# A gated-DeltaNet and Fourier layer in fp32: the scans' state update as 64-row products, in place of one product over a zero-padded operand

## The chip, the cores and the metric

One core of one Trainium2 chip runs the whole layer in one launch. The metric is the device time of that launch in microseconds, as the median of several runs.

## The reference, cut to what matters

The layer joins a bidirectional gated DeltaNet group (4 heads, head size 128) and a Fourier group, and ends in a SwiGLU FFN. It runs on 2048 sample tokens and 128 prompt tokens. The part that the change touches is the scan over chunks of 64 tokens, run forward and backward:

```python
def step(s, inp):
    u_v_c, w_c, qg_c, aqk_c, kd_c, gl_c = inp
    u = u_v_c - jnp.einsum('bhck,bhkv->bhcv', w_c, s)
    o = jnp.einsum('bhck,bhkv->bhcv', qg_c, s) + jnp.einsum('bhij,bhjv->bhiv', aqk_c, u)
    s = gl_c[..., None, None] * s + jnp.einsum('bhck,bhcv->bhkv', kd_c, u)
    return s, o
```

Per head, the state `s` is 128 x 128; the last product sums over the 64 tokens of a chunk. There are 32 chunks of the sample and 2 of the prompt, in each of two directions.

## The kernel before

`phase_ab` makes projections, convolutions and the per-chunk operands, and leaves them in DRAM. `scan1` and `scan2` run the scans, `phase_d` the FFN. A framework records the operations, then a scheduler orders them on each engine by its own model, and adds the semaphore waits; so the order in the program text is not the order on the engines.

**The scans.** `steps` goes through the steps: 2 over the prompt, 16 in `scan1`, 16 in `scan2`. One step takes one chunk of the forward direction (d = 0) and one of the backward direction (d = 1). `chunk_step` loads the chunk's operands (`pk` holds keys, queries, values and `kt`, the keys with tokens on the partitions; `ab` and `tb` are block-diagonal tiles for two heads) and returns two generators `pair(q)`. A pair is two heads, laid side by side on the 128 partitions: tokens of the first head on partitions 0 to 63 (`lo`), of the second on 64 to 127 (`hi`). `steps` advances the four generators of a step stage by stage, and after each stage calls `beside`, which records some of the other work that runs next to the scans (the Fourier transforms in `scan1`, the output projection in `scan2`); after the step `fill` records a piece of the triangular inversion.

**One pair.** It has one PSUM bank `ps` of tag `m` (four such banks exist, and a step takes all four), cut into `b0`, `b1`, `bu` and `bo` of 128 columns each.

- Stage 1: two products of the states with keys and queries into `b0` and `b1`; DVE makes `r` from them, ACT makes the first part of the output (`part`).
- Stage 2: the product `bu` from `tb` and `r`; ACT copies it out as `u`, and, scaled by `ed`, into the padded operand `rd`.
- Stage 3: the state product of `kt` and `rd` into `b0` and `b1` together, the product `bo` of `ab` and `u`; DVE forms the new states (`S`) and adds `bo` to the output.

The padded operand is one of the tiles `bd[d, "r", q]` (`bd0r`, `bd1r` in the profile), 128 x 2 x 128. The scaled `u` of the first head fills the `lo` half of its first 128 columns, that of the second head the `hi` half of its second 128 columns, and the rest stays zero from a memset at the start of `scan1`. So one product with the 128 rows of `kt` gives both heads' updates:

```python
self.act(rd[lo, 0], bu[lo], AF.Copy, scale=ed[lo])
self.act(rd[hi, 1], bu[hi], AF.Copy, scale=ed[hi])
...
self.mm(ps[:, :2 * P], kt[:, q], rd.rearrange("p h v -> p (h v)"))
```

All operations go through helpers, so the profile gives the helpers' lines: L124 is every product (`mm`), L127 a transpose, L130 `tensor_tensor`, L137 `scalar_tensor_tensor` (`r` and `S`), L140 every ACT operation, L849 and L854 the memsets of the `bd` tiles and of the states.

## Time and profile before

| what | value |
|---|---|
| runs (three) | median 2767.01 us, 2766.07 to 2773.3 |
| the profiled execution | 2767.64 us, its span 2765.8 us |
| granted TensorE clock | 0.971 of full speed over the span |
| busy | PE 94%, PEld 86%, DVE 71%, ACT 50%, POOL 13% |
| DMA | 390.83 MB, mean 141 GB/s |
| the scans | about 756 to 1263 us of the span |

The profile is of one execution. PE is the product itself, PEld the loading of its stationary operand, which runs beside products. A product over fp32 operands shows as two rows each (two passes). The ends of products are modelled, their starts are recorded; so the distance between two starts says what a product took, and a busy share near 100% says only that products followed each other.

### The profile page before, as it was taken

What the parts mean: (1) busy time and instruction counts of PE and PEld (TensorE: products, weight loads), DVE (VectorE), ACT (ScalarE), POOL (GpSimd) and SP (SyncE); (2) the same over time, 40 slices, a digit from 0 to 9 for tenths busy, and PEclk for the clock granted to TensorE, in tenths of its full rate; (3) what the DMA queues carried; (4) which work ended last, traced back from release to release, by engine and by line L of the source; (5) the groups of instructions that cost most, each with busy time, mean ns of one, the idle gap of its engine ahead of it and who ended that gap; (6) DMA issues with size and microseconds to landing.
All of it is one profiled execution on the core that took longest, in us unless ns stands there. A gap on an engine that the chain in (4) does not pass through costs nothing.

```text
span 2765.8 us, 44580 instructions
## 1 busy us (share of the span) xinstructions
PE 2610.3 (94%) x15769; PEld 2366.6 (86%) x15769; DVE 1971.7 (71%) x3860; ACT 1395.2 (50%) x3090; POOL 354.4 (13%) x486
## 2 busy tenths in 40 slices
PE   6999798899999899997999999999999999999998
PEld 3898687788888778876999998789999888999987
DVE  6335598998999677755877766577777556888744
ACT  7756454432277877765433344433434444444442
POOL 1214333431200012220000000020000002000001
PEclk8999898899999999998999999999999999999999
DMA  9946685555365666644322223532222253332342
GB/s 311 307 139 204 177 256 162 157 164 180 109 193 194 195 176 195 200 152 151 90 73 73 73 71 94 179 122 77 73 69 70 89 158 120 105 88 82 95 137 93
DMA packets 412283, 390.83 MB, mean 141 GB/s; under 512 B 99948, under 2 KB 335900, under 8 KB 411164
## 3 DMA queue, kind: packets, MB, share of 16 engines
q1 hardware_dynamic: 323996, 300.92, 36.1%
q10 hardware_dynamic: 74128, 40.13, 5.0%
q0 software_dynamic: 13936, 46.93, 4.9%
q8 instruction: 125, 2.05, 0.3%
q14 instruction: 98, 0.80, 0.1%
HBM read 293.55 MB, written 94.33 MB: 140 GB/s over the span
## 4 chain that ended last, share of the span: by engine, by line
issue 31%; PE 27%; DMA 2%; DVE 1%; ACT 1%; POOL 1%; ACTq 0%; POOLq 0%; SPq 0%; DVEq 0%
PE acc L124 9%; PE m L124 8%; PE acc L1273 5%; PE m L1273 5%; PE tr L127 1%; POOL rstd L130 1%; DMA z_s<-z_d 0%; DMA y_f<-half_d 0%; DMA half_d<-gy 0%; DVE x_f L137 0%; ACT h L140 0%; DVE x_f L130 0%; DMA bd1a<-a_d 0%; POOL y L1401 0%; DMA g<-gate_d 0%
## 5 line engine op out<-in xcount | busy, mean ns | idle before, releaser
L1273 PE MATMUL m<-h,wh 128*128 128x384 f32 (+1 forms) x1848 | 456.1, 329 | 14.5 <-ACT h L140 7.2
L1273 PE MATMUL acc<-h,wh 128*128 128x384 f32 (+1 forms) x1848 | 449.8, 327 | 0.0
L140 ACT ACTIVATE wh<-S 128x512 fp32r<-128x512 f32 x264 | 163.8, 630 | 376.5 <-DVE S L130 161.5
L124 PE MATMUL acc<-hb,w_in 128*128 128x258 f32 (+1 forms) x2304 | 333.6, 302 | 15.7 <-DMA hb<-hT 10.9
L1273 PEld LDWEIGHTS m<-h,wh 128*128 128x128 f32 x1848 | 328.4, 189 | 19.6 <-ACT h L140 8.9
L124 PEld LDWEIGHTS acc<-hb,w_in 128*128 128x128 f32 x2304 | 318.3, 199 | 26.8 <-issue 12.2
L1273 PEld LDWEIGHTS acc<-h,wh 128*128 128x128 f32 x1848 | 327.2, 189 | 1.0 <-ACT wh L140 0.4
L1273 PE MATMUL acc<-h,wl 128*128 128x384 f32 (+1 forms) x924 | 300.6, 327 | 6.0 <-DVE wl L130 6.0
L1273 PE MATMUL m<-h,wl 128*128 128x384 f32 (+1 forms) x924 | 302.3, 328 | 0.0
L140 ACT ACTIVATE wh<-w_gu 128x512 fp32r<-128x512 f32 x198 | 124.4, 630 | 118.8 <-issue 51.6
L130 DVE TENSOR_TENSOR wl<-S,wh 128x512 fp32r<-128x512 f32 x264 | 179.0, 686 | 5.3 <-ACT wh L140 3.1
L1273 PEld LDWEIGHTS acc<-h,wl 128*128 128x128 f32 x924 | 174.0, 189 | 6.9 <-DVE wl L130 6.9
L1273 PEld LDWEIGHTS m<-h,wl 128*128 128x128 f32 x924 | 174.9, 189 | 0.0
L140 ACT ACTIVATE awh<-a 128x384 fp32r<-128x384 f32 x176 | 90.7, 520 | 136.0 <-PE m L124 88.1
L130 DVE TENSOR_TENSOR awl<-a,awh 128x384 fp32r<-128x384 f32 x176 | 96.6, 555 | 87.1 <-ACT awh L140 87.0
L1387 POOL DMA_DIRECT2D half_d<-gy x17 | 9.3, 546 | 1160.9 <-DVE gy L130 1160.3
L130 DVE TENSOR_TENSOR wl<-w_gu,wh 128x512 fp32r<-128x512 f32 x198 | 135.4, 685 | 27.2 <-ACT wh L140 27.0
L130 DVE TENSOR_TENSOR S<-w_gu 128x512 f32<-128x512 f32 x132 | 91.1, 691 | 88.4 <-DMA w_gu<-w_gu 87.9
L137 DVE SCALAR_TENSOR_TENSOR y<-conv_in,wconv,y 128x256 f32<-128x256 f32 (+1 forms) x216 | 123.2, 584 | 39.7 <-ACT conv_in L140 39.1
L130 POOL TENSOR_TENSOR w_ada<-w_raw,w_ada 128x512 fp32r<-128x512 f32 x64 | 99.2, 1566 | 136.9 <-ACT w_ada L140 136.7
L124 PE MATMUL acc<-woh,mh 128*128 128x512 f32 x272 | 113.2, 419 | 3.0 <-DVE gx L130 2.9
L130 DVE TENSOR_TENSOR inv_b<-inv_b,inv_m 128x62 f32<-128x62 f32 (+30 forms) x124 | 114.1, 920 | 2.3
(281 smaller groups left out, 5927.9 us busy)
## 6 DMA issues: line engine op xcount, KB each, us to landing
w_gu<-w_gu SPq DMA_DIRECT2D x264, 256.0 KB
pk<-pk_d SPq DMA_DIRECT2D x68, 512.0 KB
w_dn<-w_down SPq DMA_DIRECT2D x132, 256.0 KB
hb<-hT SPq DMA_DIRECT2D x104, 258.0 KB
w_raw<-w_ada SPq DMA_DIRECT2D x32, 512.0 KB
x<-x SPq DMA_DIRECT2D x17, 512.0 KB
hT<-hi ACTq DMA_DIRECT2D x17, 512.0 KB
hT<-lo POOLq DMA_DIRECT2D x17, 512.0 KB, 6.1
```

The source lines that it names most:

```text
L124: self.nc.tensor.matmul(out, lhsT=lhsT, rhs=rhs, start=start, stop=stop)
L127: self.nc.tensor.transpose(out=out, in_=in_, identity=self.c("ident")[:in_.shape[0], :in_.shape[0]])
L130: (eng or self.nc.vector).tensor_tensor(out=out, in0=a, in1=b, op=op)
L137: self.nc.vector.scalar_tensor_tensor(out=out, in0=a, scalar=s, in1=b, op0=op0, op1=op1)
L140: self.nc.scalar.activation(out=out, in_=in_, func=f, **kw)
L1273: nc.tensor.matmul(o, lhsT=w_[:, ws], rhs=h_[:, k, :sub], start=start and k == i == 0, stop=k == 3 and i == 2, skip_group_check=not start)
L1387: nc.gpsimd.dma_start(self.half_d[n], tmp)
```

## The change

The state product is split by head. ACT now writes one unpadded 128 x 128 tile `rd`. Two products of 64 rows follow, one per head: the first takes partitions 0 to 63 of `kt` and `rd`, the second partitions 64 to 127, so that each uses one half of the array's rows. They write different banks: `grown` takes, for both pairs of a direction, the first head's result from the bank of the first pair and the second head's from the bank of the second pair, at the columns `b0` for the first pair and `b1` for the second. The product `bo`, the new states and the output's additions move into a fourth stage. `steps` runs four stages, and calls `beside` after the first three as before. The padded tiles and their four memsets are gone.

```diff
@@ -843,7 +843,7 @@
         self.ts(self.e2, self.qs, P * EPS, ALU.mult, P * EPS * 1e-6, ALU.add)
         self.bd = {}
         for d in range(2):
-            for kind, count, m in (("a", 3, 2), ("t", 2, 4), ("r", 2, 2)):
+            for kind, count, m in (("a", 3, 2), ("t", 2, 4)):
                 for n in range(count):
                     t = self.bd[d, kind, n] = oacc.tile([P, m, P], F32, name=f"bd{d}{kind}{n}")
                     nc.gpsimd.memset(t, 0.0)
@@ -882,10 +882,11 @@
 
         for slot, *cs in steps:
             heads = [h for d, c in enumerate(cs) for h in self.chunk_step(d, c, slot)]
-            for stage in range(3):
+            for stage in range(4):
                 for h in heads:
                     next(h, None)
-                self.beside(us[stage])
+                if stage < 3:
+                    self.beside(us[stage])
             self.fill(8.0)
 
     def chunk_step(self, d, c, slot):
@@ -912,9 +913,12 @@
         o = self.o_tiles[c]
         lo, hi = slice(0, CH), slice(CH, P)
 
+        banks = []
+
         def pair(q):
             s0, s1 = self.states[d, 2 * q], self.states[d, 2 * q + 1]
             ps = self.bank("m")
+            banks.append(ps)
             b0, b1, bu, bo = (ps[:, i * P:(i + 1) * P] for i in range(4))
             self.mm(b0, kq[:, q, 0], s0)
             self.mm(b1, kq[:, q, 1], s1)
@@ -929,14 +933,16 @@
             yield
             self.mm(bu, tb[:, q], r)
             u = sp.tile([P, P], F32, tag=f"u{d}{q}", name="u", bufs=1)
-            ed, rd = self.ed[:, d, q, c:c + 1], self.bd[d, "r", q]
-            self.act(rd[lo, 0], bu[lo], AF.Copy, scale=ed[lo])
-            self.act(rd[hi, 1], bu[hi], AF.Copy, scale=ed[hi])
+            rd = sp.tile([P, P], F32, tag=f"rd{d}{q}", name="rd", bufs=1)
+            self.act(rd, bu, AF.Copy, scale=self.ed[:, d, q, c:c + 1])
             self.act(u, bu)
             yield
-            self.mm(ps[:, :2 * P], kt[:, q], rd.rearrange("p h v -> p (h v)"))
+            grown = [bank[:, q * P:(q + 1) * P] for bank in banks]
+            for dst, hs in zip(grown, (lo, hi)):
+                self.mm(dst, kt[hs, q], rd[hs])
+            yield
             self.mm(bo, ab[:, q], u)
-            for h2, (st, src) in enumerate(((s0, b0), (s1, b1))):
+            for h2, (st, src) in enumerate(zip((s0, s1), grown)):
                 new = sp.tile([P, P], F32, tag=f"S{d}{2 * q + h2}", name="S")
                 self.stt(new, st, self.gl[:, h2, d, q, c:c + 1], src, ALU.mult, ALU.add)
                 self.states[d, 2 * q + h2] = new
```

The scheduler's order of PE in one step of `scan2`, with buffer numbers. Before: `m_11908` is the bank of direction 0's first pair, `m_11917` that of its second; `bd0r0` and `bd0r1` are their padded operands, `acc` the output projection that runs beside.

```order
L124 MATMUL m_11908<-bd0r0_8494,pk_11900 128x256 [waits Activation_49]
L124 MATMUL m_11908<-u_12009,bd0a0_8484 128x128 [waits DMAHW2_49,DMAHW1_49]
L124 MATMUL acc_12191<-woh4_9739,mh_11972 128x512 [waits DVE_49]
L124 MATMUL acc_12191<-wol4_9747,mh_11972 128x512
L124 MATMUL acc_12191<-woh4_9739,ml_11973 128x512
L124 MATMUL acc_12191<-woh5_9740,mh_11972 128x512
L124 MATMUL acc_12191<-wol5_9748,mh_11972 128x512
L124 MATMUL m_11917<-bd0r1_8496,pk_11900 128x256 [waits Activation_49]
L124 MATMUL m_11917<-u_12014,bd0a0_8484 128x128
```

Of the change, in a step of `scan2`: `m_11992` is the bank of the first pair, `m_12001` of the second; `rd_12094` belongs to the first pair, `rd_12099` to the second. What goes to `m_11992` is a first head's product, what goes to `m_12001` a second head's; `tr` are transposes beside.

```order
L124 MATMUL m_11992<-rd_12099,pk_11984 128x128 [waits Activation_49]
L124 MATMUL m_12001<-rd_12094,pk_11984 128x128 [waits Activation_49]
L124 MATMUL m_12001<-rd_12099,pk_11984 128x128
L124 MATMUL m_11992<-u_12093,bd0a0_8484 128x128 [waits DMAHW5_49,DMAHW3_49]
L127 MATMUL tr_12264<-const_all_73,xn_12153 128x128
L124 MATMUL acc_12279<-wol0_9775,mh_12056 128x512
L124 MATMUL m_12019<-r_12022,bd1t0_8500 128x128 [waits DVE_49,Activation_49]
L124 MATMUL m_12010<-rd_12104,pk_11988 128x128 [waits Activation_49]
```

One product with its `bo` behind it has become two first halves apart from each other (that of the first pair stands some ten rows further up), two second halves in a row behind the second pair's `u`, and `bo` of the first pair behind all of them.

DVE at the same places, the new states `S` and the output `o`. Before:

```order
L137 SCALAR_TENSOR_TENSOR S_12054<-S_11835,gl_2171,m_11908 128x128 [waits PE_49]
L137 SCALAR_TENSOR_TENSOR S_12056<-S_11837,gl_2171,m_11908 128x128
L130 TENSOR_TENSOR o_10025<-o_10025,m_11908 128x128
L137 SCALAR_TENSOR_TENSOR S_12062<-S_11843,gl_2171,m_11917 128x128 [waits PE_49]
L137 SCALAR_TENSOR_TENSOR S_12064<-S_11845,gl_2171,m_11917 128x128
L130 TENSOR_TENSOR o_10025<-o_10025,m_11917 128x128
```

The change:

```order
L137 SCALAR_TENSOR_TENSOR S_12182<-S_11959,gl_2171,m_12001 128x128 [waits PE_49,Activation_49]
L137 SCALAR_TENSOR_TENSOR S_12180<-S_11957,gl_2171,m_11992 128x128 [waits PE_49]
L130 TENSOR_TENSOR o_10065<-o_10065,m_11992 128x128
L137 SCALAR_TENSOR_TENSOR S_12187<-S_11964,gl_2171,m_11992 128x128
L134 TENSOR_SCALAR h_12147<-tr_12264,mod_cols_81 128x128 [waits PE_49]
L134 TENSOR_SCALAR h_12147<-tr_12264,mod_cols_81 128x128
L130 TENSOR_TENSOR gx_12156<-acc_12279,g1_11320 128x512 [waits PE_49]
L130 TENSOR_TENSOR ml_12507<-mf_12508,mh_12506 128x512 [waits DMAHW3_49,Activation_49]
L130 TENSOR_TENSOR x_c_12062<-x_c_12062,gx_12156 128x512 [waits DVE_49]
L137 SCALAR_TENSOR_TENSOR S_12189<-S_11966,gl_2171,m_12001 128x128 [waits PE_49]
L130 TENSOR_TENSOR o_10065<-o_10065,m_12001 128x128
```

The states of one pair came in a row, each pair from its own bank; now the second head's state of the first pair comes first, and the last state, `S_12189`, waits for a later product of PE.

PE between the two, in the change: `u_12098` is the second pair's `u`.

```order
L124 MATMUL acc_12384<-woh4_9771,mh_12283 128x512
L124 MATMUL acc_12384<-wol4_9779,mh_12283 128x512
L124 MATMUL acc_12384<-woh4_9771,ml_12284 128x512
L124 MATMUL acc_12384<-woh5_9772,mh_12283 128x512
L124 MATMUL acc_12384<-wol5_9780,mh_12283 128x512
L124 MATMUL m_12001<-u_12098,bd0a0_8484 128x128 [waits DVE_49]
```

Its product `bo` waits for DVE, which has to read a state's update out of the same bank first; before, this product had no wait on DVE.

## Rows read from the trace of the kernel before

**Rows 1.** Page, section 1: busy us of each engine (share of the span) xinstructions.

```profile
PE 2610.3 (94%) x15769; PEld 2366.6 (86%) x15769; DVE 1971.7 (71%) x3860; ACT 1395.2 (50%) x3090; POOL 354.4 (13%) x486
```

**Rows 2.** Scan stretch by window: length, busy PE, PEld, DVE, ACT, POOL (x), clock, DMA, GB/s.

```profile
756.00:800.00 44.00, 36.38 (x242) 33.06 (x243) 40.85 (x83) 28.56 (x80) 5.63 (x15) 0.92 0.76 209
800.00:870.00 70.00, 67.57 (x465) 60.52 (x464) 68.28 (x168) 54.39 (x154) 0.22 (x1) 1.00 0.60 186
870.00:960.00 90.00, 82.29 (x518) 70.56 (x518) 66.86 (x205) 79.89 (x217) 1.43 (x2) 1.00 0.66 207
960.00:1020.00 60.00, 52.25 (x294) 43.74 (x292) 41.90 (x136) 44.47 (x133) 8.01 (x16) 0.97 0.62 170
1020.00:1200.00 180.00, 178.48 (x1004) 154.58 (x1005) 124.78 (x374) 134.39 (x397) 43.48 (x84) 1.00 0.61 188
```

**Rows 3.** By window, of instructions on `bd0r` alone: PE, PEld, ACT, POOL.

```profile
870.00:1020.00 150.00, 17.09 (x52) 8.24 (x52) 18.83 (x52) 0.00 (x0) 0.99 0.65 192
980.00:1015.00 35.00, 5.57 (x18) 2.81 (x18) 5.44 (x15) 0.00 (x0) 1.00 0.74 205
1050.00:1190.00 140.00, 8.31 (x28) 5.12 (x28) 10.54 (x30) 0.00 (x0) 1.00 0.63 193
```

**Rows 4.** Timeline of PE: start us, length us, line, output<-inputs, weights, moving, passes.

```profile
803.29 0.60 PE L124 MATMUL m<-bd1r,pk 128*128 128x256 f32 x2
803.72 0.38 PE L124 MATMUL m<-u,bd1a 128*128 128x128 f32 x2
...
804.39 0.83 PE L124 MATMUL acc<-w_fno,const_fourier 128*128 128x128 f32 x6
805.06 0.39 PE L124 MATMUL m<-r,bd0t 128*128 128x128 f32 x2
805.38 0.63 PE L124 MATMUL tr<-const_fourier,uv 32*128 32x32 f32 x4
805.93 0.49 PE L124 MATMUL m<-r,bd0t 128*128 128x128 f32 x2
806.26 0.61 PE L124 MATMUL m<-S,pk 128*128 128x128 f32 x4
```

**Rows 5.** The same, around a product with 32 columns of weights.

```profile
843.17 0.61 PE L124 MATMUL acc<-const_fourier,uv 128*128 128x128 f32 x4
843.71 0.65 PE L124 MATMUL tr<-cw,rc 128*32 128x256 f32 x2
844.29 0.49 PE L124 MATMUL acc<-const_fourier,uv 128*128 128x128 f32 x2
```

**Rows 6.** Groups by form, 756 to 1263: xcount | busy us, mean ns | idle before.

```profile
L137 DVE SCALAR_TENSOR_TENSOR S<-S,gl,m 128x128 f32<-128x128 f32 x272 | 81.9, 341 | 17.7 <-PE m L124 6.0 <-ACT o L140 4.0 <-ACT u L140 1.9
...
L140 ACT ACTIVATE bd0r<-m,ed 64x128 f32<-64x128 f32 x136 | 49.2, 362 | 12.6 <-PE m L124 9.8 <-PE acc L124 0.6
...
L124 PE MATMUL m<-bd0r,pk 128*128 128x256 f32 x136 | 42.5, 394 | 5.5 <-ACT u L140 5.2
...
L140 ACT ACTIVATE u<-m 128x128 f32<-128x128 f32 x136 | 37.8, 278 | 1.9
```

**Rows 7.** Timeline of PE, products of column halves (`m<-kq`).

```profile
259.02 1.15 PE L124 MATMUL m<-kq 128*64 128x128 f32 x24
260.11 0.40 PE L124 MATMUL m<-w_ada,cs 128*4 128x512 f32 x1
```

**Rows 8.** Timeline of PE behind a wait, in a bare step.

```profile
940.52 0.70 PE L124 MATMUL m<-bd0r,pk 128*128 128x256 f32 x2 [0.26 <-ACT u L140]
941.06 0.38 PE L124 MATMUL m<-u,bd0a 128*128 128x128 f32 x2
```

**Rows 9.** Tile `pk`, 756 to 1263: engines idle before its instructions until, us, times.

```profile
  ACT u L140: 21.3, 46
```

**Rows 10.** Timeline at the start of the scans, POOL and DVE.

```profile
757.09 1.31 POOL L854 MEMSET S<- 128x128 f32 x7
...
761.59 0.71 DVE L137 SCALAR_TENSOR_TENSOR r<-m,nsr,pk 64x128 f32<-64x128 f32 x2
```

## The prediction

> **What bounds the kernel now.** I read the page's busy shares first, then the scan stretch alone, because the change touches only `chunk_step`. PE is busy 94% of the span and no other engine passes 71% [rows 1]; its busy figures are modelled, so I use the distance between the starts of neighbouring products instead. The scans run from about 756 to 1263 us. The windows split this stretch [rows 2]: from 1020 to 1200 PE is busy 178.48 of 180 us while ACT and DVE have 134.39 and 124.78, so there the time is PE's stream and nothing else. From 800 to 870 PE (67.57 of 70) and DVE (68.28 of 70) share the bound, from 870 to 960 PE (82.29 of 90) and ACT (79.89 of 90). From 960 to 1020 PE has 8 us free, and the chain of one scan step shows: the products of the padded operand come 18 passes in 35 us from 980 on [rows 3], four per step and direction, so a bare step each 7.8 us; from 1050 to 1190 it is 28 passes in 140 us, a step each 20 us.
>
> **The units.** A product over fp32 shows as two passes. Starts of neighbouring full-array groups give the price of a pass: six passes of 128 columns take 805.06 - 804.39 = 0.67 us, 0.11 each; a state update of before, two passes of 256 columns, takes 803.72 - 803.29 = 0.43 us [rows 4].
>
> **What leaving the full array costs.** The kernel of before already has products that use part of the array. In [rows 4] the product of 32 rows (`tr<-const_fourier,uv`) stands between two full ones. From the full product ahead of it (805.06) to the one two places behind it (806.26) eight passes go by, 0.89 us at 0.11 each; the clock shows 1.20. So one trip out of the full array and back costs 0.31 us: about 0.10 on the way in (0.32 instead of 0.22), 0.11 over the four passes and the way out (0.55 instead of 0.44), and 0.11 on the first full product behind it (0.33 instead of 0.22). A product with 32 columns of weights shows the same in [rows 5]: 0.54 instead of 0.45 ahead of it, 0.58 instead of 0.43 (two passes of 256 columns) through it and out. The Trainium skill says of this, in TensorEngine Tiling, Key Properties, that changing the tiling mode drains the engine; it gives no figure, and the rows here agree with it and supply one.
>
> **The change part by part.**
>
> 1. *The state product on PE.* 136 products of 128 rows and 256 columns (34 steps x 2 directions x 2 pairs; 136 passes in [rows 6] for direction 0, as many for the other) become 272 of 64 rows and 128 columns. In the order of the changed program they stand in 186 groups between full-array products: 114 first halves alone, 50 groups of two second halves, 15 of a first half and two second ones, 7 others. The two products of one group of second halves use the same half of the array. Each group is a trip: 186 x 0.31 = 57.7 us more for PE.
> 2. *The streaming itself.* No row shows 64 rows by 128 columns. The nearest are the 128-column passes, 0.11 each: two halves one behind the other take 2 x 0.22 = 0.44 against 0.43, so 136 x 0.01 = +1.4 us. Only where a first and a second half are neighbours (18 places) can they run side by side and save 0.22 each, 4.0 us. That parts of the array can run side by side is seen on column halves: 24 passes of `m<-kq` (8 of 128 columns, 16 of 64) would take 8 x 0.11 + 16 x 0.055 = 1.76 us one behind the other and are through in 1.09 [rows 7]. Net -2.6 us.
> 3. *Trips that are partly paid already.* Behind a wait PE's first product is slow in any case: 941.06 - 940.52 = 0.54 instead of 0.43 [rows 8]. PE waited for ACT's `u` ahead of products with `pk` 46 times, 21.3 us in all [rows 9]; there the way in costs nothing new: -46 x 0.10 = -4.6 us.
>    PE's stream therefore grows by 57.7 - 2.6 - 4.6 = 50.5 us.
> 4. *What of it lies on the path.* 80 of the 186 trips belong to the 16 steps of `scan2`, nearly all in the saturated stretch: 50.5 x 80 / 186 = 21.7 us, taken whole. The other 28.8 us fall into 756 to 1020 us, where PE has about 25 us without work and DVE, ACT and the chain set the end in turn [rows 2]; I take half, 14.4 us (ends: nothing and all). On the path: 36.1 us.
> 5. *ACT.* Two copies of 64 rows at 362 ns become one of 128 rows, priced as its neighbour `u` of the same shape, 278 ns [rows 6]: 0.45 us less per pair, 136 x 0.45 = 61 us of ACT. Where PE is the bound this is worth nothing. It is worth at most the 21.3 us for which PE waited on ACT ahead of these products [rows 9]. But the second halves now wait for `u` of the second pair (the order below the diff shows it), so I take a third: -7 us (ends: 0 and -21).
> 6. *New waits.* The product `bo` of the second pair now waits for DVE's update of a state in its bank, 68 times; before none waited for DVE. One update takes 341 ns [rows 6]. Where other products stand between (Fourier, outputs) it costs nothing; in the five or so bare steps [rows 3], two waits each, 10 x 0.34 = +3 us (ends: 0 and 68 x 0.34 = 23). Queued behind such a wait is all of PE, since its products go in order; the next step's products wait for the state that comes after it.
> 7. *Memsets and the fourth stage.* Four POOL memsets fewer, ahead of the states' own memsets [rows 10]. DVE's first operation of a scan starts at 761.59 us, 3.2 us after the last state memset has ended, behind the inversion's products; that covers it, so nothing; without that cover it would be about the 1.3 us that seven memsets of half the size took. Stage four calls no `beside`, so the work handed out beside a step is the same, and no DMA is added or moved in the program text.
>
> Sum: 36.1 - 7 + 3 = +32 us. The profiled execution took 2767.64 us (span 2765.8), 0.6 us from the median of the runs, 2767.01. 2767.6 + 32 = 2800 us.
>
> **Rivals.**
>
> - *The halves run side by side and the trips cost nothing: faster.* The Trainium skill, TensorEngine Tiling, Overview and Key Properties, promises up to twice the speed for a contraction of at most 64 rows, since tiles load weights and multiply in parallel. As a mechanism of this kernel: each pair saves 0.43 - 0.22 = 0.21 us of PE, 136 x 0.21 = 28.6 us; by the weights of step 4 (43% whole, 57% half) 20.4 us come through, with ACT's 7 us: 2740 us. It decides only if first and second halves stand side by side, and if the trip of [rows 4] were an affair of 32-row products. For it speaks [rows 7]; against it that 18 of 136 pairs stand so in the order. Chance 0.10.
> - *ACT's relief pays for the trips: no change.* From 870 to 1020 us ACT is as busy as PE or the chain is bare; about 13 steps lie there (52 passes of `bd0r` at four a step [rows 3]), 52 pairs x 0.45 = 23.4 us gained if each step shortens by its copies, the trips before 1020 vanish in idle time, and 21.7 us remain in `scan2`: about 2766 us. For it speaks ACT's 79.89 of 90 us [rows 2]; against it that PE was just as busy there. Chance 0.18.
> - *The banks tie the pairs together: much slower.* Both pairs now write each other's bank, so a second half waits for the other pair, and `bo`, the state update and the next step follow in file. If all of PE's growth and all 68 waits lie on the path: 50.5 + 23 = +73 us, 2841 us; half of the excess over my forecast is enough to reach 2820. It decides where a step's chain, 7.8 us in the bare steps, is as long as the work beside it; in `scan2` a step takes 20 us [rows 3], which speaks against it. Chance 0.10.
>
> **How the numbers follow.** My forecast, trips on a saturated PE, has 0.62 and by itself covers 2779 (the early trips cost nothing, ACT gives half of its 21.3 us, the new waits nothing: 21.7 - 10.7) to 2821 (all of them cost, ACT gives nothing: 50.5 + 3). Within 0.3%, 8.3 us, is about what a measurement of this kernel can tell from no change. Faster by more has the first rival and a little of the second: 0.12. Within it most of the second and the forecast's lower edge: 0.15. Slower: the rest of the forecast, the third rival and the second's upper tail: 0.73. The range of 2758 to 2824 takes in the forecast and the second rival; it leaves out the first and most of the third, 2 in 10.
>
> **What would show it.** Right: between a product with `rd` and the next full one about 0.2 us from start to start more than the passes need, and a slow first pass behind it; `scan2` longer by some 20 us and PE still busy from end to end in it; the copies to `rd` at about 278 ns; ACT's busy time 61 us lower without gain; the stages ahead of 750 and behind 1300 us as before. Wrong: halves that start a few ns apart and no gap behind them (first rival); an unchanged length of `scan2`; or PE standing idle ahead of `bo` and the second halves, which would be the third rival. The scheduler also moves products in the stages that the change does not touch; a shift of more than some 5 us there would be outside my account.

## The result, and the profile after

The changed kernel takes 2831.12 us (median of four runs, 2825.72 to 2832.58), the kernel before 2767.26 beside it: a ratio of 1.0223, 95% interval 1.0202 to 1.0243, or +62 us (56 to 67). The profiled execution took 2832.58 us with a span of 2830.7. Below, "us" of a comparison are ratio differences times 2767, since each ratio is taken beside runs of the kernel before on the same chip; between two experiments they are good to some 6 us.

The page of the changed kernel, section 1 (beside [rows 1]):

```profile
PE 2681.4 (95%) x16041; PEld 2397.3 (85%) x16041; DVE 1977.9 (70%) x3860; ACT 1329.6 (47%) x2956; POOL 346.0 (12%) x482
```

PE has 71 us more, the weight loads beside it (PEld) 31 more, ACT 66 us less, the others nothing of note. PE's timeline of the kernel before, of the changed kernel, at the first product of `scan2` and at the first product behind the scans, shows where the time lies:

```profile
992.50 0.61 PE L124 MATMUL m<-S,pk 128*128 128x128 f32 x4
...
1303.57 0.69 PE L1273 MATMUL m<-h,wh 128*128 128x384 f32 x1 [3.85 <-ACT h L140]
```

```profile
1030.65 0.49 PE L124 MATMUL m<-S,pk 128*128 128x128 f32 x2
...
1366.60 0.69 PE L1279 MATMUL m<-h,wh 128*128 128x384 f32 x1 [4.67 <-ACT h L140]
```

At the start of `scan2` the changed kernel is 38 us late, behind the scans 63; `scan2` takes 336.0 us instead of 311.1. The span is 65 us longer, so little of note happens elsewhere. The windows of the changed kernel (columns as in [rows 2]):

```profile
756.00:800.00 44.00, 38.44 (x198) 31.67 (x197) 33.86 (x59) 17.48 (x50) 7.17 (x21) 0.81 0.71 197
800.00:870.00 70.00, 70.00 (x476) 60.67 (x475) 63.27 (x162) 44.07 (x126) 1.83 (x3) 1.00 0.51 152
870.00:960.00 90.00, 85.70 (x512) 70.29 (x510) 62.94 (x164) 55.16 (x154) 1.43 (x2) 0.94 0.62 191
960.00:1060.00 100.00, 91.12 (x512) 70.72 (x511) 62.03 (x208) 53.11 (x178) 7.87 (x16) 0.98 0.55 154
1060.00:1260.00 200.00, 199.20 (x1103) 161.73 (x1101) 128.84 (x375) 114.38 (x353) 41.04 (x81) 1.00 0.57 171
```

ACT is now far from the bound everywhere (55.16 of 90 us from 870 on, where [rows 2] had 79.89), and from 800 to 870 PE leaves no gap: it had shared that stretch with DVE. So PE became the bound in the early stretch too.

**What a trip costs.** PE's timeline of the changed kernel, in `scan2`:

```profile
1195.48 0.49 PE L124 MATMUL m<-rd,pk 64*128 64x128 f32 x4
1195.90 0.49 PE L124 MATMUL m<-r,bd1t 128*128 128x128 f32 x2
1196.32 0.49 PE L124 MATMUL m<-rd,pk 64*128 64x128 f32 x2
1196.74 0.49 PE L124 MATMUL m<-u,bd0a 128*128 128x128 f32 x2
1197.06 0.27 PE L127 MATMUL tr<-const_all,xn 128*128 128x128 f32 x1
...
1203.05 0.39 PE L124 MATMUL acc<-wol,mh 128*128 128x512 f32 x1
1203.28 0.40 PE L124 MATMUL acc<-woh,ml 128*128 128x512 f32 x1
1203.60 0.71 PE L124 MATMUL m<-rd,pk 64*128 64x128 f32 x6
1204.25 0.49 PE L124 MATMUL m<-u,bd1a 128*128 128x128 f32 x2
```

From 1195.90 to 1197.06, 1.16 us, six passes go by, which take 0.67 at full pace; 0.49 are left, and 0.10 of them are the tail of the trip before. (The 0.32 from `u` to `tr`, for two passes of 0.11, shows such a tail.) One trip costs 0.39 us. Its parts, as medians of the distances between the starts of single passes (205, 213, 202 and 213 ns where full passes stand 112 apart): 0.09 into the small tile, 0.10 between its first pass and its second, 0.09 out, and 0.10 behind the first full pass.

The second piece shows side by side: a first half and two second halves, six passes, are through in 0.65 us with the way out. One behind the other they would take 0.67 + 0.10 + 0.09 = 0.86. Such groups start two passes 7 ns apart, as the single starts show, and cost 0.18 us instead of 0.39.

The groups by form in the scans of the changed kernel (columns as in [rows 6]):

```profile
L124 PE MATMUL m<-rd,pk 64*128 64x128 f32 x544 | 111.5, 323 | 1.0 <-ACT rd L140 1.0
...
L137 DVE SCALAR_TENSOR_TENSOR S<-S,gl,m 128x128 f32<-128x128 f32 x272 | 90.3, 345 | 83.5 <-PE m L124 56.2 <-issue 10.0 <-ACT o L140 8.2
...
L140 ACT ACTIVATE rd<-m,ed 128x128 f32<-128x128 f32 x136 | 50.1, 368 | 44.9 <-PE m L124 41.4 <-DVE x_c L130 1.8
L140 ACT ACTIVATE u<-m 128x128 f32<-128x128 f32 x136 | 37.1, 273 | 0.1
```

The direction of the waits has turned. Before, PE waited 5.2 us for ACT's `u` ahead of the state product of one direction, and DVE waited 6.0 us for PE ahead of `S` [rows 6]. Now PE waits 1.0 us ahead of the 544 passes, while DVE waits 56.2 us for PE and ACT 41.4: everybody waits for TensorE. And PE's own wait for `S`, which the new order of `bo` adds, is short; the table of waits has

```profile
PE m L124 <- DVE S L137: 4.4, 9, 1.1
```

### The profile page after: what moved, and what is told of

Read it like the earlier page. It is cut to its first block, busy times and chain, and to the rows that moved or that the text cites. A ratio compares the mean times of both kernels' runs of the same rounds, so it can differ in the third digit from the quotient of the medians.

```text
span 2830.7 us, 44880 instructions
## 1 busy us (share of the span) xinstructions
PE 2681.4 (95%) x16041; PEld 2397.3 (85%) x16041; DVE 1977.9 (70%) x3860; ACT 1329.6 (47%) x2956; POOL 346.0 (12%) x482
## 4 chain that ended last, share of the span: by engine, by line
PE 56%; DVE 3%; DMA 2%; ACT 1%; issue 1%; POOL 0%; SPq 0%; DVEq 0%; POOLq 0%; ACTq 0%
PE acc L1279 16%; PE m L1279 15%; PE acc L124 13%; PE m L124 11%; PE tr L127 1%; DMA y_f<-half_d 1%; DVE S L130 0%; DVE x_f L137 0%; DVE x_f L130 0%; DVE h L130 0%; POOL rstd L130 0%; DVE wl L130 0%; DMA h_d<-h 0%; DMA w_gu<-w_gu 0%; DMA h<-h_d 0%
## 5 line engine op out<-in xcount | busy, mean ns | idle before, releaser
L1279 PE MATMUL m<-h,wh 128*128 128x384 f32 (+1 forms) x1848 | 454.9, 328 | 14.6 <-ACT h L140 8.3
L137 DVE SCALAR_TENSOR_TENSOR S<-S,gl,m 128x128 f32<-128x128 f32 x272 | 90.3, 345 | 83.5 <-PE m L124 56.2
```

What stands on the lines that cost most here:

```text
L137: self.nc.vector.scalar_tensor_tensor(out=out, in0=a, scalar=s, in1=b, op0=op0, op1=op1)
L1279: nc.tensor.matmul(o, lhsT=w_[:, ws], rhs=h_[:, k, :sub], start=start and k == i == 0, stop=k == 3 and i == 2, skip_group_check=not start)
```

## The experiments

Theory A: the 186 trips make the loss. Theory B: the fourth stage, the crossed banks and the new waits lengthen a scan step. The runs walk from the kernel before to the changed one, and then try to gather the trips. In the diffs, names are those of `chunk_step` and `steps`.

| run | ratio to before | 95% interval | us |
|---|---|---|---|
| two_full | 1.0040 | 1.0025 to 1.0055 | +11 |
| one_half_small | 1.0096 | 1.0081 to 1.0111 | +27 |
| full_rows | 1.0042 | 1.0027 to 1.0057 | +12 |
| padded_4stage | 1.0076 | 1.0059 to 1.0093 | +21 |
| one_copy_3stage | 0.9991 | 0.9977 to 1.0005 | -2 |
| full_rows_3stage | 0.9991 | 0.9981 to 1.0002 | -2 |
| own_bank_4stage | 0.9956 | 0.9941 to 0.9971 | -12 |
| own_bank_one_small | 1.0099 | 1.0084 to 1.0114 | +27 |
| before_4stage | 0.9974 | 0.9965 to 0.9983 | -7 |
| padded_keys | 1.0014 | 1.0004 to 1.0024 | +4 |
| padded_keys_4stage | 1.0011 | 1.0002 to 1.0020 | +3 |
| u_first | 1.0129 | 1.0111 to 1.0147 | +36 |
| full_rows_u_first | 1.0037 | 1.0025 to 1.0050 | +10 |
| four_gathered | 1.0068 | 1.0048 to 1.0088 | +19 |
| four_gathered_late | 1.0029 | 1.0017 to 1.0041 | +8 |
| eight_gathered | 1.0275 | 1.0254 to 1.0297 | +76 |
| full_rows_5_banks | 1.0143 | 1.0121 to 1.0166 | +40 |
| own_bank_5_banks | 1.0096 | 1.0081 to 1.0111 | +27 |

**full_rows: the changed kernel without its trips.**

```diff
-                self.mm(dst, kt[hs, q], rd[hs])
+                self.mm(dst, kt[:, q], rd)
```

> The changed kernel with both state products of a pair taken over all 128 rows of the one unpadded copy (each state then receives both heads' updates: that part of the computation is changed). Stages, banks, copies, waits and the streaming time stay as in the changed kernel; only the way out of the full array is gone. Theory A (the 186 trips out of the full array, 0.39 us each, are the whole loss): 2755 to 2780 us. Theory B (the fourth stage, the crossed banks and the waits of bo on VectorE lengthen the chain of a scan step): 2815 to 2835 us. Half and half would read 2795 to 2805.

2780.45 us, just past theory A's range: 1.0042. The trips are worth 1.0223 - 1.0042, 50 us of the 62. PE's timeline of this run shows a state product that costs its two passes, 0.22, and nothing around it:

```profile
1193.74 0.38 PE L124 MATMUL m<-r,bd1t 128*128 128x128 f32 x2
1193.96 0.39 PE L124 MATMUL m<-S,pk 128*128 128x128 f32 x2
1194.19 0.39 PE L124 MATMUL m<-rd,pk 128*128 128x128 f32 x2
1194.41 0.39 PE L124 MATMUL m<-S,pk 128*128 128x128 f32 x2
```

Here `scan2` runs from 999.74 to 1310.87, 311.1 us. So of the 50 us about half, 336.0 - 311.1 = 24.9, belongs to its 80 trips, the rest to the 106 trips ahead of it.

**padded_4stage: the two half copies back.**

```diff
-            self.act(rd, bu, AF.Copy, scale=self.ed[:, d, q, c:c + 1])
+            self.act(rd[lo, 0], bu[lo], AF.Copy, scale=ed[lo])
+            self.act(rd[hi, 1], bu[hi], AF.Copy, scale=ed[hi])
...
-                self.mm(dst, kt[hs, q], rd[hs])
+                self.mm(dst, kt[:, q], rd[:, h2])
```

> The changed kernel's four stages and two crossed banks, but with the zero-padded operand and its two half copies on ScalarE back, each half a product of its own over 128 rows. Against the run with full rows and one copy it has only the additional ScalarE time, 136 times 0.36 us = 49 us. Theory A with ScalarE off the path: 2760 to 2785 us, within 10 us of the run with full rows. If the relief of ScalarE was worth much and hid part of the loss: 2790 to 2830 us. Theory B (stages and banks): 2815 or more.

2787.42 us, 9 us above full_rows: ScalarE's relief, 68 us of busy time (1396.1 here, 1327.7 in full_rows), goes with a gain of about 9. The half copies also bring another order of the other products (below), so the 9 us are not ScalarE's alone.

**one_half_small and two_full: trips put into the kernel before, and their control.**

```diff
-            self.mm(ps[:, :2 * P], kt[:, q], rd.rearrange("p h v -> p (h v)"))
+            self.mm(b0, kt[lo, q], rd[lo, 0])
+            self.mm(b1, kt[:, q], rd[:, 1])
```

The control has `self.mm(b0, kt[:, q], rd[:, 0])` in place of the first.

> The kernel before, three stages, own banks, two half copies, padded operand, with one edit: the 256-column state product is two, the first of 64 rows by 128 columns, the second of 128 rows by 128 columns. It leaves the full array 134 times and changes nothing else of note (0.44 for 0.43 us of streaming). Theory A: 134 trips at 0.39 us, all on the path, 52 us, so 2815 to 2830 us. At the prediction's price and share (0.31 us, 0.63 of it on the path) 26 us: 2790 to 2798. Theory B: the trips are nearly free, 2765 to 2775.

> The control of the run before: the kernel before with its 256-column state product as two products of 128 rows by 128 columns. No trips, the same streaming. Every theory: 2762 to 2778 us; what the run with one small half has above this one is the price of 134 trips, 48 to 56 us by theory A.

The control gave 2779.28 us, 1 us over its range, and the run with trips 2794.25: 15 us, far below theory A's 48 to 56. The expectation counted 134 trips; on TensorE 136 first halves stand alone between full products, and the common trip has its 0.39 us in the trace too (the same 205, 213, 202 and 213 ns). A trip's price on TensorE and its price in time are two things; own_bank_one_small, below, comes back to this. That the mere split into two products costs 11 us was in no theory.

**The order of the other products, a rival for the small differences.** The scheduler orders all products anew for each program. By an alignment of the orders on TensorE, about half of the 2600 passes of the scans stand at another place in two_full than in the kernel before, a third in before_4stage, and three quarters in full_rows against own_bank_4stage. So the 11 us here, and every difference below whose two programs differ in more than the rows of a product, hold a change of order that no run separates. The price of the trips is free of this: full_rows, two_full and own_bank_4stage have the order of their partners with trips.

**one_copy_3stage, own_bank_4stage, full_rows_3stage: stage and banks one by one.** With full_rows they are the four corners of a square: own or crossed banks, three or four stages, always one copy, two products over 128 rows and no trip. The first is the kernel before with

```diff
-            self.act(rd[lo, 0], bu[lo], AF.Copy, scale=ed[lo])
-            self.act(rd[hi, 1], bu[hi], AF.Copy, scale=ed[hi])
+            self.act(rd, bu, AF.Copy, scale=self.ed[:, d, q, c:c + 1])
...
-            self.mm(ps[:, :2 * P], kt[:, q], rd.rearrange("p h v -> p (h v)"))
+            self.mm(b0, kt[:, q], rd)
+            self.mm(b1, kt[:, q], rd)
```

own_bank_4stage adds to it a `yield` ahead of `bo` and the changed kernel's loop in `steps`; full_rows_3stage takes both away from full_rows.

> The kernel before (three stages, each pair in its own bank) with one copy of 128x128 in place of the two half copies and two products over all 128 rows of it (each state then receives both heads' updates: that part of the computation is changed). It has ScalarE's relief and the split into two products, but no trip, no fourth stage and no crossed banks. From the runs so far: the split is worth +11 us, ScalarE's relief -7, the fourth stage with crossed banks +8. If these add up: 2768 to 2777 us, some 8 under the run with full rows. If the fourth stage and the crossed banks cost nothing: 2778 to 2784, like the run with full rows.

> The run with one copy and three stages, with bo and the additions behind it put into a fourth stage, as the changed kernel has it; every pair stays in its own bank (each state still receives both heads' updates, that part of the computation is changed). No trip, no crossed bank. The run with full rows, which has the fourth stage and the crossed banks, stood 18 us above the run with neither. If the fourth stage makes that: 2776 to 2785 us. If the crossed banks make it: 2759 to 2767. If each makes a part: between.

> The run with full rows, with the fourth stage undone: the two pairs' banks stay crossed, but bo and the additions follow the state products at once (each state still receives both heads' updates, that part of the computation is changed). If the fourth stage makes the 18 us: 2759 to 2768 us. If the crossed banks make them: 2776 to 2785.

| | three stages | four stages |
|---|---|---|
| own banks | 0.9991 | 0.9956 |
| crossed banks | 0.9991 | 1.0042 |

Neither edit costs anything by itself, which none of the expectations had: by ratio the fourth stage is a gain of 10 us with own banks (medians 2759.31 and 2762.49 us, taken on different chips; the second is 6 us under its ranges), the crossing costs nothing with three stages. Together they cost 24 us against own banks with four stages. The groups by form show what is later; of full_rows, then of own_bank_4stage:

```profile
L137 DVE SCALAR_TENSOR_TENSOR r<-m,nsr,pk 64x128 f32<-64x128 f32 x272 | 94.4, 347 | 22.1 <-PE m L124 19.4
```

```profile
L137 DVE SCALAR_TENSOR_TENSOR r<-m,nsr,pk 64x128 f32<-64x128 f32 x272 | 94.7, 348 | 14.3 <-PE m L124 10.0 <-DMA bd0t<-t_d 0.4
```

DVE's first operation of a step waits 9 us more for the products of that step. These need a free bank, and a crossed bank is read by both pairs before it comes free; the runs with five banks try that. Another order of the other products is a possible cause too.

**own_bank_one_small: trips without crossed banks.**

```diff
-            self.mm(b0, kt[:, q], rd)
+            self.mm(b0, kt[lo, q], rd[lo])
```

> The run with own banks and four stages (2759 us), with its first product of a pair taken over 64 rows: the first state is then right, the second still receives both heads' updates. 123 groups leave the full array, at 0.39 us each 47 us of TensorE, and no bank is crossed. By the share that the changed kernel showed against the run with full rows (50 of 69 us): 34 us, 2789 to 2800. By the share of the run with one small half on three stages (15 of 52): 14 us, 2769 to 2778. If the trips only cost when the banks are crossed: 2762 or less.

2791.22 us, in the first range; by ratio, 1.0099 against 0.9956, 40 us. So the trips do not need the crossed banks. The expectation counted 123 groups of state products; each first half leaves the full array by itself, 136 times, also where two pairs follow each other. At 0.39 us that is 53 us of TensorE, 0.29 us of time for each.

**How much of a trip becomes time.** In three pairs of programs the engines have the same instructions in the same order (but for up to four passes ahead of the scans), and only the rows of products differ. So the starts on TensorE can be subtracted pass by pass, in us:

| pair | trips | TensorE at 0.39 | longer around the trips | all else | span | by ratio |
|---|---|---|---|---|---|---|
| two_full, one_half_small | 136 | 53 | 38 | -23 | 16 | 15 |
| own_bank_4stage, own_bank_one_small | 136 | 53 | 49 | -22 | 27 | 40 |
| full_rows, changed kernel | 186 | 69 | 59 | -1 | 58 | 50 |

(69 is 186 x 0.39 less 0.21 for each of 18 groups with halves side by side. A span is one execution, so it differs from the ratio by up to 13 us.) Of a trip, a part goes under where TensorE had waited anyway: 15, 4 and 10 us. Another part is made up by shorter waits at other products: 22 to 23 us in the first two pairs. In the third 13 us come back in this way at the full clock, and stretches at the lower of the two clock levels, 1.2 GHz, take 12 again. The runs show it too: their granted clock is 0.9695 in the median, that of full_rows 0.973, which makes 173 us at that level against 150. As passes there take about twice as long (207 ns for 105, at eight_gathered below), some 11 of the 50 us are, by this estimate, time at the lower clock. Only the trips differ between the two programs, but what brought the clock down is not shown, and a part of the time at it lies ahead of the scans (92 us against 85 in the profiles).

**u_first and full_rows_u_first: fewer trips by ScalarE's order.**

```diff
-            self.act(rd, bu, AF.Copy, scale=self.ed[:, d, q, c:c + 1])
             self.act(u, bu)
+            self.act(rd, bu, AF.Copy, scale=self.ed[:, d, q, c:c + 1])
```

> The changed kernel with the two copies of a pair on ScalarE in the other order, u ahead of rd. The first pair's H product, which waits for the second pair's u to be read, is then free as early as the second pair's L product, and the program leaves the full array 134 times and not 186: 64 times for one product alone, 62 times for three that run partly side by side. Theory A, by groups: 64 at 0.39 and 62 at about 0.18 us, 38 us in all for 69, and of the 31 us less some three quarters on the path: 2802 to 2812 us. If the loss does not hang on the trips: 2825 to 2835.

> The run with full rows (2780 us: crossed banks, four stages, no trips; each state receives both heads' updates) with the copies on ScalarE in the other order, u ahead of rd, so that no H product waits for a later u. If the crossed banks' 24 us (against own banks, 2759) come from that wait: 2758 to 2768 us. If they come from something else in the crossing: 2776 to 2784. The same edit took 33 us off the changed kernel, 24 of them expected from fewer trips; what falls here falls there too.

u_first: 2797.96 us by median, 4 us under theory A's range; by ratio 26 us under the changed kernel, with 52 trips fewer and half of the first halves beside second ones. The same edit without trips is worth 1 us (1.0037 against 1.0042). So the 26 us are trips, and the second half's wait for the other pair's `u` isn't what the crossed banks cost.

**full_rows_5_banks and own_bank_5_banks: a spare bank.**

```diff
-            with self.psum(4, 2, 2):
+            with self.psum(5, 2, 1):
```

> The run with full rows (crossed banks, four stages, no trips; each state receives both heads' updates) with five banks for the scans' pairs in place of four, taken from the transposes, which keep one of two. With four banks a step's four pairs hold them all, and a crossed bank comes free only when both pairs have read their states and outputs. To be read against the next run, which has the same banks and no crossing. If the 24 us of the crossing are the wait for a free bank: 0 to 10 us above the next run. If not: 16 to 32 us above it.

> The run with own banks and four stages (each state receives both heads' updates), also with five banks for the pairs and one for the transposes. The single transpose bank may cost both runs time, by the same amount; 2755 to 2790 us. What the run before stands above this one is the price of the crossing with a bank to spare.

2807.86 and 2791.81 us: 13 us apart by ratio, 16 by median, between what the two readings wanted. With the single bank for transposes one is 28 us slower than with two, the other 39, not the same amount, so the pair decides little. That a crossed bank comes free later is perhaps a part of the 24 us; what the rest is stays open.

**four_gathered, four_gathered_late, eight_gathered: one trip for several products.** The products of the two pairs of a direction are collected and issued one right behind the other, second and first halves in turn; order edges tie each of them to the first:

```diff
-            for dst, hs in zip(grown, (lo, hi)):
-                self.mm(dst, kt[hs, q], rd[hs])
+            self.grow.append([(dst, kt[hs, q], rd[hs]) for dst, hs in zip(grown, (lo, hi))])
+            if len(self.grow) == 2:
+                lead = None
+                for pair_of in self.grow:
+                    for dst, w, x in pair_of[::-1]:
+                        with self.tc.issue_after(lead.ins) if lead else nullcontext():
+                            ins = self.nc.tensor.matmul(dst, lhsT=w, rhs=x, start=True, stop=True)
+                        lead = lead or ins
+                self.grow = []
```

eight_gathered collects the four pairs of both directions, with an edge from each product to the one ahead. four_gathered_late offers the other work of a step behind the fourth stage (`if stage != 2` for `if stage < 3`).

> The changed kernel with the four state products of a direction's step issued one right behind the other, H and L in turn, so that two run side by side: 70 trips, 66 of them of four products. By the group of three seen in the changed kernel, such a group should take 0.84 us from the last full product to the next at its own pace, against 0.89 for its eight passes one by one. Theory A: the trips then cost nothing, and the time is that of the run with full rows or some us less, 2770 to 2785 us. Rival: the first L product is held back until the second pair's copies are done, and that wait lengthens each step of the chain by 0.3 to 0.6 us per direction: 2795 to 2820.

> The run with four products gathered, with one edit: the other work of a step (the place where Fourier and output products are offered) comes after the fourth stage and no longer between the state products and bo. 72 trips. If the fourth stage lengthens a step because other products come between the state products and bo: 2765 to 2776 us, 7 to 18 under the run with four gathered. If the place of the other work does not matter: 2778 to 2788, as there.

> The same with all eight state products of a step, both directions, in one group: 35 trips. By the same pace a group takes about 1.29 us for 1.78 us of passes one by one, 17 us less of TensorE than the run with full rows. Theory A: 2760 to 2778 us, down to the kernel before or under it. Rival: a direction now waits for the other's copies, and the chain of each step grows by more than TensorE is relieved: 2785 to 2830.

2782.82, 2777.11 and 2840.10 us. With four in a group the trips are all but paid (7 us above full_rows, at the upper end of theory A's range), and with the other work moved the kernel is level with full_rows (4 us under it) and 8 us above the kernel before; its time lies between its two ranges, so whether the place of the other work matters is open. PE's timeline of four_gathered (`mm` is L125 here) has eight passes in 0.64 us with the way out, for 0.89 one by one:

```profile
1162.78 0.38 PE L125 MATMUL m<-r,bd1t 128*128 128x128 f32 x2
1163.10 0.71 PE L948 MATMUL m<-rd,pk 64*128 64x128 f32 x8
1163.74 0.50 PE L125 MATMUL acc<-wol,mh 128*128 128x512 f32 x1
```

With eight the price is the wait: windows and PE's waits of eight_gathered,

```profile
960.00:1060.00 100.00, 78.03 (x480) 64.26 (x478) 57.77 (x194) 48.56 (x163) 6.32 (x13) 0.85 0.48 145
1060.00:1260.00 200.00, 185.48 (x1029) 152.49 (x1030) 119.72 (x350) 106.44 (x330) 39.32 (x75) 0.91 0.51 157
...
PE m L125 <- ACT o L141: 17.5, 33, 2.6
PE m L948 <- ACT u L141: 13.6, 14, 2.6
```

PE stands idle for 22 of 100 us where the changed kernel had 9. It waits 13.6 us for `u` ahead of a group and 17.5 us for ACT's `o` (4.5 in the changed kernel). In these stretches the granted clock averages 0.85 and 0.91 of full speed where the changed kernel had 0.98 and 1.00: part of the time goes at the lower level, 1.2 GHz. 13 of the 35 groups run at it, with 207 ns from one couple of passes to the next instead of 105. Over the whole run the clock is 0.9595, by estimate 80 us more at the lower level than in full_rows, which would be 40 of the 64 us between the two. That the waits bring the clock down was not tried apart.

**before_4stage, padded_keys, padded_keys_4stage: what of the change is worth keeping.** The first is the kernel before with nothing but the `yield` ahead of `bo` and the loop of four stages. The others keep one copy and full-array products by padding the keys:

```diff
-        pk = sp.tile([P, 1024], F32, tag=f"pk{d}", name="pk")
-        nc.sync.dma_start(pk, self.pk_d[c])
+        pk = sp.tile([P, 768], F32, tag=f"pk{d}", name="pk")
+        nc.sync.dma_start(pk, self.pk_d[c][:, :768])
+        kz = self.bd[d, "k", slot % 2]
+        for h in range(2):
+            hs = slice(h * CH, (h + 1) * CH)
+            nc.sync.dma_start(kz[hs, 2 * h:2 * h + 2], self.pk_d[c][hs, 768:].rearrange("p (q k) -> p q k", q=2))
...
+            self.mm(b0, kz[:, q], rd)
+            self.mm(b1, kz[:, 2 + q], rd)
```

> The kernel before with one edit: bo and the additions behind it go into a fourth stage, as in the changed kernel. Padded operand, half copies, one product of 256 columns and own banks stay, and so does all that is computed. With one copy the fourth stage was worth 0.35% (ratio 0.9956 against 0.9991). If it is worth that here too: 2756 to 2762 us beside a kernel before at 2767. If it only pays together with ScalarE's relief: 2764 to 2770. Slower than before would say that the stage is part of the changed kernel's loss.

> The kernel before, its computation whole, with the zeros on the other side of the state product: the keys of the two heads are loaded into zero-padded tiles by two DMAs more per chunk, one 128x128 copy on ScalarE takes the place of the two half copies, and two products over 128 rows by 128 columns give the two states. Three stages, own banks, no trip. If ScalarE's relief is what the run with one copy and three stages showed and the two further DMAs are hidden: 2758 to 2768 us, at or some us under the kernel before. If the DMAs of 64 KB each come late: 2775 to 2800.

> The run with padded keys with the same fourth stage, its computation whole. If the stage is worth 0.35% here too: a ratio of 0.996 to 1.000 (2757 to 2767 us beside 2767). If the two further DMAs per chunk set the pace: 1.001 to 1.004, as with three stages.

before_4stage takes 2757.23 us, 0.9974: 7 us faster than the kernel before, more than its interval. Its first product behind the scans starts at 1297.44 instead of 1303.57:

```profile
1297.44 0.69 PE L1275 MATMUL m<-h,wh 128*128 128x384 f32 x1 [4.07 <-ACT h L140]
```

padded_keys and its four-stage form (2773.72 and 2768.48) are 6 and 15 us slower than one_copy_3stage and own_bank_4stage: 1.0014 against 0.9991, 1.0011 against 0.9956. They differ from these by two DMAs more per chunk, four more tiles to clear, the weights' place and the order of the other products; which of these makes the 6 to 15 us is open.

## Why the prediction was right and wrong

The mechanism and the direction held: trips out of a busy TensorE, slower. The time was 31 us too low, and the walk of the runs says where. From the kernel before: fourth stage alone -7 (before_4stage), one copy and two products -5 (own_bank_4stage), crossed banks on four stages +24 (full_rows), halves and their trips +50 (changed kernel); sum +62. The forecast had 36 for the trips, where 50 came, and +3 for banks and stage together (steps 6 and 7), where 24 - 7 = 17 came: the two misses are equal, 14 us each. Only the first has a cause that runs with the same order show.

Steps 3 and 5 use the time for which TensorE waited for `u` before. Its products (PE) and its weight loads (PEld) have each their own line there:

```profile
PE m L124 <- ACT u L140: 6.7, 15, 0.7
...
PEld m L124 <- ACT u L140: 14.6, 31, 0.9
```

- **Step 1, the price of a trip, failed in size:** 0.31 us was forecast, 0.39 measured. The product of [rows 4] has another shape, 32 rows and 32 columns. By its single starts its first pass is followed by the second after 0.13 us; with 64 rows and 128 columns it is 0.21. That makes the missing 0.08 us. The count, 186, held.
- **Step 2** held where halves are neighbours (0.21 us saved for each of 18 groups, forecast 0.22). That two products in place of one cost 1.4 us is not borne out: two_full shows 11, order included.
- **Step 3** rests on a wrong reading: [Rows 9] adds both kinds. Paid by a wait were 15 entries by PE's count or 31 by that of the weight loads, not 46: 1.5 to 3.1 us, not 4.6. What went under around the trips in the changed kernel was 10 us all the same, 59 for 69; the growth forecast was 50.5.
- **Step 4, the share:** 36.1 of 50.5 was forecast, 0.71; 50 of 59, 0.85, came. For `scan2`, 21.7 us were forecast and 24.9 came. The half taken for the early trips was too little: 14.4 forecast, some 25 measured. PE's free time there [rows 2] was taken as cover, but from 800 to 870 the changed kernel has none left.
- **Step 5:** -7 forecast, -9 (full_rows against padded_4stage) to -14 (one_copy_3stage against two_full) measured, with the order's part in both. It is near by luck. The bound of 21.3 us is the wrong reading of step 3; it should have been 6.7 to 14.6. The copy lasts 368 ns, not 278, since `u` has no scale and `rd` has one; by such lengths a pair saves 0.36 us, not 0.45. But the next ACT instruction starts 375 ns behind the start of a half copy and 266 behind that of the whole one (medians), so a pair saves 0.48 us, 66 in all, as ACT's busy time shows. The 61 us named as a sign was close because the two errors cancel.
- **Steps 6 and 7 failed, by as much as the trips.** The wait of `bo` for DVE was priced, at +3, and is small (4.4 us). What lay beside it was not: crossed banks and a fourth stage, each free alone, cost 24 us together, and step 7 held the stage for nothing in either direction. The cause of the 24 us is open. The memsets' zero was not tried apart.

Of the rivals, the third (banks that tie the pairs together) had the mechanism for these 24 us and a time near the result, 2841; but the sign that it named, PE idle ahead of `bo`, is not there, and the larger part is trips. The first needed halves side by side: the gathered runs show that they do run so, and that even then the kernel gets no faster, since the zeros of the padded operand cost TensorE only 0.21 us per pair and the gathering has its own waits. The second, ACT's relief, was worth 9 to 14 us at most where it needed 23, and the early trips did not vanish. The sign named for the forecast, about 0.2 us from `rd` to the next full product and a slow pass behind it, is in the rows.

The Trainium skill, TensorEngine Tiling, Key Properties, says that a change of the tiling mode drains the engine. The trace agrees and gives the size: 0.39 us for out and back at full clock. Its promise of up to twice the speed for a contraction of at most 64 rows (the same page, Overview) is seen here only inside a group: eight passes 0.64 us instead of 0.89.

## What to carry to other kernels

Count how often a change takes TensorE out of its full array, at 0.39 us each as measured here, before counting the multiplications by zero that it saves: 0.21 us per pair could not pay for one trip of its own. Where small tiles are wanted, issue four or so in one go, halves in turn, but only those whose inputs are ready together. Make a restructuring one edit at a time: the part of this change that was meant as a mere rearrangement, the fourth stage, is a gain of 7 us alone and takes part in a loss of 24 with the rest. Where a scheduler orders the program, look for a partner with the same order of instructions: only there is a difference the edit's own.

## What the runs showed of the hardware that was not expected

- The first pass of a product of 64 rows and 128 columns is followed by its second only after 0.21 us, for 0.11 in the full array; and so is the first full pass behind the trip. Behind the first pass of 32 rows and 32 columns it is 0.13.
- Passes on the two halves of the array start 7 ns apart when they stand side by side in the stream and write different banks.
- A ScalarE copy of 128x128 with a scale per row takes 368 ns, one of 64x128 with a scale 361 to 362, one of 128x128 without a scale 273 to 278: here the scale cost some 95 ns, the rows nearly nothing. What counts on a busy engine is another number: the next instruction starts 266 ns behind the start of the whole copy with a scale, and 375 ns behind that of a half copy, so two halves took 0.75 us.
- The same trip cost 0.11 us of the kernel's time with three stages and two half copies (15 us for 136), and 0.29 with four stages and one copy (40 us for 136).
